# Weight buffers from one tile, handed out by the kernel, and the experts' weights in 2 MB transfers

## The chip, the cores and the metric

The kernel runs on one core of a Trainium2 chip. The metric is the device time of one execution in microseconds (us); the time shown is the median of three runs.

## The reference

The model takes x, one sequence of 256 tokens with 1024 features, in float32, through two blocks of two layers each.

First block, for layer 0 and 1 (ALPHA is the square root of 2):

```
m = conv_mixer(x)  (layer 0)   or   rglru_mixer(x)  (layer 1)
x = layer_norm(ALPHA * x + m, ln1)
f = moe(x)                     # 16 experts, the best 2 of each token, in one of 4 groups
x = layer_norm(ALPHA * x + f, ln2)
```

`conv_mixer` is a product with w_in, two causal depthwise convolutions with gates, and a product with w_out. `rglru_mixer` is u = x w_in, split into a branch y and xr; a causal convolution of 4 taps over xr; two gates, each a block diagonal product of xr; a linear recurrence over the tokens; and (gelu(y) h) w_out. An expert is (silu(x w1) * (x w3)) w2, where w1, w3 and w2 are 1024 x 1024, so an expert has 12 MB of weights, and a layer 192 MB. Every expert's weights are used.

Second block: forgetting attention with 16 heads, a convolutional FFN of width 2816, dilated attention in three groups, the FFN again, and a last rms_norm.

## The kernel before

The 256 tokens stay in SBUF through the whole program, and all the weights, some 547 MB, pass through once. TensorE (PE) works on them in the order of the model: conv mixer, experts of layer 0 (their first product at 117 us), recurrence mixer (from 567), experts of layer 1 (from 678), second block (from about 1135). The order of instructions on each engine is the order in which the kernel's text issues them (a manual schedule): an instruction that waits holds up all that stand behind it on its engine. What a buffer's next writer waits for is the buffer's last reader, by semaphores that the framework places.

Weights. `make_plan` (L352) lists all pieces of 1 MB (128 partitions with a row of 8 KB each) in the order of use. `Ring` (L213) has 19 buffers of one piece each (`SLOTS`), from a tile pool that hands them out in rotation; pieces and larger activations (`take`) share them. `pump` issues the next load on SyncE's queue (SP, L243) as long as a buffer is free in program order; the load itself waits on the chip until the buffer's last reader is done. `reserve` buffers stay free for activations that are yet to come. During the experts, where the parts of `Splitter` aren't needed, their tiles are lent as four pairs of half pieces (`spare`, L236: two loads of 512 KB with rows of 4 KB), and go back and forth until the experts end.

Products outside the experts are split: `Splitter` (L274) makes two parts of each half piece, L293 on ScalarE (ACT) casts the high part and L294 on VectorE (DVE) subtracts for the low part, and PE multiplies three times (L499 to L501). Some pieces are used whole (L495). At most three halves are split ahead.

Experts. `moe` (L1286) sorts tokens by one-hot products. Per expert, stage1 (L1215) reads 8 pieces (w1 and w3, two column halves), stage2 (L1241) the other 4 (w2). Piece n of expert e is key ("moe", l, e, n); `done` frees it after its last reader. Ahead of expert 12 stands a branch for experts with more than 64 tokens (not taken here), which costs PE a jump. The gain and offset of the next norm are spread over the partitions at expert 10 (ln1) and 14 (ln2) into a buffer `gb` (`spread`), which `affine` (L742) later reads on GpSimd (POOL): L745 multiplies by the gain and L746 adds the offset, for each half of the tokens, and then the buffer is dropped.

Between the experts of layer 0 and the recurrence mixer, `go` (L414) takes a buffer for x, three for xT (`split_fm`, L593: the normalized x, feature-major, as two parts and whole) and calls `affine(x, gb, x)`. Then `rglru` begins:

```
            xr, rt, av = view(), view(), view()      # L962: three buffers of the ring
            ...
            conv(products(0))                        # chunks 0 and 1
            conv(products(2))
            pair = products(4)
            conv(pair)
            gates(0)
            gates(1)
```

`products(c)` makes two chunks of 128 columns in PSUM (four tiles `m` in rotation) and L974 on ScalarE writes xr[:, c] from it; `conv` adds three taps to each on VectorE (six L982), then casts (L987, ScalarE) and subtracts (L988, GpSimd); `gates` (L1000 to L1002) needs these and PSUM tiles that the taps have left.

Of the kernel before, what the change touches and what calls it, by code (L numbers as in the profile page):

```python
# [22 lines left out]
SLOTS = 19  # L23
# [32 lines left out]
def wide(w):  # L56
    """[1024, C] -> pieces [2 * C / 512, 128, 4 * 512]: 512 columns, half of the rows."""
# [78 lines left out]
def alibi():  # L136
    """[8, 128, 1152]: per head, the score bias of the three dilated groups."""
# [22 lines left out]
def layout(inp):  # L160
# [52 lines left out]
class Ring:  # L213
    """Slots of 8 KB per partition: weight pieces of 1 MB, loaded in the order in which they are read, and the
    larger activations. `reserve` slots stay free of pieces for activations that are yet to come. `spare`: pairs of
    [128, 1024] tiles that can take the experts' pieces."""

    def __init__(self, nc, pool, plan):
        self.nc, self.pool, self.plan = nc, pool, plan
        self.next, self.used, self.reserve, self.tiles, self.spare = 0, 0, 0, {}, []  # L220

    def slot(self, dtype=F):
        assert self.used < SLOTS
        self.used += 1
        return self.pool.tile([128, 2048], dtype, name="w", tag="w")

    def pump(self):
        while self.next < len(self.plan):
            key, src, n, dst = self.plan[self.next]
            if self.used + self.reserve >= SLOTS:  # L230
                if not self.spare or key is None or key[0] != "moe":
                    break
                self.next += 1
                self.tiles[key] = t = self.spare.pop(0)
                for b in range(2):
                    self.nc.sync.dma_start(t[b], src[:, b * 1024:(b + 1) * 1024])  # L236
# [1716 lines left out]
```

## Time and profile before

| | |
|---|---|
| runs | 1800.62, 1799.11, 1800.96 us; median 1800.62 |
| profiled execution, first to last instruction (its span; no other time of it is given) | 1801.5 us, mean granted TensorE clock 0.986 |
| PE busy | 1739.3 us, 97% of the span, 11892 matmuls |
| VectorE, ScalarE, GpSimd busy | 786.0, 579.5, 210.9 us |
| read from memory | 547.25 MB, 304 GB/s over the span |
| matmuls of the experts, L1215 and L1241 | 366.4 and 181.6 us |
| loads of the experts' pieces | 304 of 1 MB into ring buffers, and the rest in halves of 512 KB |

Busy time is summed over the instructions of an engine; a wait belongs to the engine that stands idle. The share of the DMA is the mean busy share of 16 engines in a stretch. Times within the execution are counted from its first instruction.

### The profile page before, as it was taken

The page shows a single profiled execution, that of the slowest core. Times are in us where ns is not written, and L with a number is a line of the kernel's source. Part 1 is how long each engine was busy: PE and PEld are TensorE (multiplying, and loading weights), DVE is VectorE, ACT ScalarE, POOL GpSimd, SP SyncE. Part 2 cuts the span into 40 slices and gives each one's busy share as a digit, 9 for nine tenths or more (in the row PEclk, how much of TensorE's full clock was granted, in tenths as well). Part 3 has the DMA queues.
Part 4 walks back from the last instruction along what each step waited for, and adds up shares of the span by engine and source line. Part 5 has one row for each costly group of instructions (what it writes and reads, how often), then busy time and mean ns, then how long its engine had stood idle before and what let it go on. Part 6 is the DMA issues. An engine that isn't in the chain of part 4 may idle for free. (4 is left out here: it accounts for less than half of the span.)

```text
span 1801.5 us, 28912 instructions
## 1 busy us (share of the span) xinstructions
PE 1739.3 (97%) x11892; PEld 1252.7 (70%) x11892; DVE 786.0 (44%) x1560; ACT 579.5 (32%) x1065; POOL 210.9 (12%) x211
## 2 busy tenths in 40 slices
PE   9999999998999989999999899899999999999998
PEld 8765555554546975555555454688999989989997
DVE  5841111111115771111111111877877776668776
ACT  5630000010003640000010000555655563456555
POOL 4500000002003300000002000300222200003222
PEclk9999999999999999999999998999999999999999
DMA  9979999999999479999999999626455233665500
GB/s 379 367 296 419 418 421 418 419 418 418 418 419 400 195 302 373 419 419 419 419 418 420 418 416 420 260 85 242 162 190 188 86 121 110 260 259 185 196 1 24
DMA packets 87964, 550.28 MB, mean 305 GB/s; under 512 B 10112, under 2 KB 10112, under 8 KB 31504
## 3 DMA queue, kind: packets, MB, share of 16 engines
q1 hardware_dynamic: 87696, 548.31, 75.6%
q8 instruction: 97, 1.59, 0.3%
q14 instruction: 43, 0.35, 0.1%
q0 software_dynamic: 128, 0.03, 0.0%
HBM read 547.25 MB, written 1.05 MB: 304 GB/s over the span
## 5 line engine op out<-in xcount | busy, mean ns | idle before, releaser
L1215 PE MATMUL m<-w,hi 128*64 128x256 f32 x3264 | 366.4, 381 | 0.0
L294 DVE TENSOR_TENSOR lo<-w,hi 128x1024 fp32r<-128x1024 f32 x238 | 303.5, 1281 | 56.0 <-ACT hi L293 54.8
L1215 PEld LDWEIGHTS m<-w,hi 128*64 128x64 f32 x3264 | 232.3, 137 | 127.8 <-issue 12.3
L499 PE MATMUL m<-w,hi 128*128 128x256 f32 x1104 | 314.4, 285 | 0.0
L500 PE MATMUL m<-w,lo 128*128 128x256 f32 x1104 | 312.7, 283 | 0.5 <-DVE lo L294 0.5
L501 PE MATMUL m<-w,hi 128*128 128x256 f32 x1104 | 312.4, 283 | 0.0
L293 ACT CAST hi<-w 128x1024 fp32r<-128x1024 f32 x232 | 240.0, 1044 | 58.3 <-PE m L501 21.4
L1222 ACT ACTIVATE h<-m 128x256 f32<-128x256 f32 x64 | 24.5, 383 | 680.1 <-PE m L1215 668.9
L1224 DVE TENSOR_TENSOR hs<-h,m 128x256 f32<-128x256 f32 x64 | 26.9, 421 | 435.2 <-ACT h L1222 435.2
L499 PEld LDWEIGHTS m<-w,hi 128*128 128x128 f32 x1104 | 211.8, 192 | 3.8 <-issue 2.1
L500 PEld LDWEIGHTS m<-w,lo 128*128 128x128 f32 x1104 | 211.8, 192 | 2.4 <-DVE lo L294 0.8
L501 PEld LDWEIGHTS m<-w,hi 128*128 128x128 f32 x1104 | 211.8, 192 | 0.0
L1241 PE MATMUL m<-w,ht 128*64 128x512 f32 x800 | 181.6, 604 | 0.2 <-DMA w<-moe 0.2
L1241 PEld LDWEIGHTS m<-w,ht 128*64 128x64 f32 x800 | 55.7, 138 | 109.3 <-issue 104.0
L1403 DVE COPY ys<-m 128x512 f32<-128x512 f32 x30 | 20.7, 692 | 236.1 <-PE m L1241 236.1
L1859 DVE SCALAR_TENSOR_TENSOR t<-u,vecs,t 128x254 f32<-128x254 f32 (+1 forms) x176 | 94.1, 592 | 0.0
L1852 ACT ACTIVATE t<-u,vecs 128x256 f32<-128x256 f32 x88 | 53.0, 602 | 113.4 <-DVE u L1846 110.8
L722 POOL DMA_DIRECT2D w<-rows x4 | 2.4, 598 | 649.5 <-DMA spare<-moe 268.8
L1326 PE MATMUL m<-d,w 128*128 128x128 f32 x512 | 64.6, 288 | 11.5 <-PEq L1348 9.9
L1326 PEld LDWEIGHTS m<-d,w 128*128 128x128 f32 x512 | 62.8, 203 | 13.5 <-issue 11.9
L1846 DVE TENSOR_TENSOR u<-m,w 128x256 f32<-128x256 f32 x84 | 35.4, 422 | 73.1 <-PE m L501 72.8
L1866 POOL TENSOR_TENSOR t<-t,t 128x256 f32<-128x256 f32 x44 | 51.6, 1174 | 123.2 <-ACT t L1865 123.2
(386 smaller groups left out, 2317.1 us busy)
## 6 DMA issues: line engine op xcount, KB each, us to landing
w<-moe SPq DMA_DIRECT2D x304, 1024.0 KB, 16.7
w<-up SPq DMA_DIRECT2D x44, 1024.0 KB, 4.9
lo<-moe SPq DMA_DIRECT2D x72, 512.0 KB, 13.9
hi<-moe SPq DMA_DIRECT2D x54, 512.0 KB, 15.1
w<-down SPq DMA_DIRECT2D x22, 1024.0 KB, 4.8
w<-b_qk SPq DMA_DIRECT2D x12, 1024.0 KB, 4.8
w<-even_in SPq DMA_DIRECT2D x9, 1024.0 KB, 14.0
spare<-moe SPq DMA_DIRECT2D x18, 512.0 KB, 10.1
```

What stands on the lines that cost most here:

```text
L293: (copy or self.nc.scalar.copy)(hi, w)
L294: self.nc.vector.tensor_tensor(lo, w, hi.bitcast(F), op=OP.subtract)
L499: mm(ps, hi[:, k], xT[0][:, k], start=k == 0, stop=False)
L500: mm(ps, lo[:, k], xT[0][:, k], start=False, stop=False)
L501: mm(ps, hi[:, k], xT[1][:, k], start=False, stop=k == 7)
L1215: nc.tensor.matmul(h[f * 64:(f + 1) * 64, j * 256:(j + 1) * 256], xg[:, 4 * i + 2 * b + k], wv[:, k, f], start=i + b + k == 0, stop=i + b ...
L1241: self.nc.tensor.matmul(y[dh * 64:(dh + 1) * 64, :], ht[:, j, f], w[:, dh * 512:(dh + 1) * 512], start=s + j + f == 0, stop=s + j + f == 3)
L1326: nc.tensor.matmul(ps[:, k], x[:, tt, kc], d[:, tt], start=tt == 0, stop=tt == 1)
L1846: nc.vector.tensor_tensor(u, ps, across, op=OP.mult)
L1852: nc.scalar.activation(t, u, AF.Identity, bias=cb[:, ch:ch + 1], scale=cw[:, ch, 2:3])
L1859: nc.vector.scalar_tensor_tensor(t[:, s:], u[:, :256 - s], cw[:, ch, 2 - s:3 - s], t[:, s:], op0=OP.mult, op1=OP.add)
L1866: nc.gpsimd.tensor_tensor(t0, t0, t1, op=OP.mult)
```

## The change

All buffers are now named by the kernel. One tile, the arena, has 15 slots of 8 KB per partition (0 to 14) side by side; slot 15 (`SINGLE`) is a tile of its own; 16 to 19 (`PAIRS`) are two tiles of two slots; 20 to 23 (`SPARE`) stand for the four tiles of `Splitter`, whose two parts now lie in one tile. That is 20 buffers, and four more while they are lent. `take(name)` gives the highest free slot of the arena, or a named slot; xT's two parts go into a pair. Loads go to the first slot in the list of free ones, but `room` holds back the highest `reserve` slots and those in `keep`.

An expert's weights are laid out as 6 blocks of 2 MB with rows of 16 KB instead of 12 of 1 MB. A block goes into two adjacent free slots in one transfer. Where no such pair is free it goes as two halves of 1 MB (`half`), until `settle(True)` at expert 1; after that only into slots that have no partner (`alone`). `settle` also ends the return of lent tiles. The last expert's w2 stays in pieces of 1 MB. Readers see the same 1024 columns at a time as before, through `quarter`, and the order of the matmuls is the same. Comments are removed; the scratch for GpSimd's DMAs has another size.

```diff
-SLOTS = 19
+SLOTS = 15
+SINGLE = 15
+PAIRS = (16, 18)
+SPARE = (20, 21, 22, 23)
...
-    m = np.empty((2, 16, 12, 128, 2048), inp["moe_w1"].dtype)
+    m = np.empty((2, 16, 6, 128, 4096), inp["moe_w1"].dtype)
     for s in range(2):
-        for i in range(2):
-            m[:, :, 4 * s + i] = w1[:, :, s, :, 4 * i:4 * i + 4].reshape(2, 16, 128, 2048)
-            m[:, :, 4 * s + 2 + i] = w3[:, :, s, :, 4 * i:4 * i + 4].reshape(2, 16, 128, 2048)
-            m[:, :, 8 + 2 * s + i] = w2[:, :, s, :, i].reshape(2, 16, 128, 2048)
+        m[:, :, 2 * s] = w1[:, :, s].reshape(2, 16, 128, 4096)
+        m[:, :, 2 * s + 1] = w3[:, :, s].reshape(2, 16, 128, 4096)
+        m[:, :, 4 + s] = w2[:, :, s].reshape(2, 16, 128, 4096)
...
     def __init__(self, nc, pool, plan):
         self.nc, self.pool, self.plan = nc, pool, plan
-        self.next, self.used, self.reserve, self.tiles, self.spare = 0, 0, 0, {}, []
-    def slot(self, dtype=F):
-        assert self.used < SLOTS
-        self.used += 1
-        return self.pool.tile([128, 2048], dtype, name="w", tag="w")
+        self.arena = pool.tile([128, SLOTS * 2048], F, name="w")
+        self.free = list(range(SLOTS + 1)) + [p + i for p in PAIRS for i in range(2)]
+        self.pairs, self.experts, self.lent, self.settled = {}, set(), False, False
+        self.next, self.reserve, self.keep, self.tiles, self.owner = 0, 0, set(), {}, {}
+        self.half = None
+    def lend(self):
+        self.free += SPARE
+        self.lent = True
+        self.pump()
+    def settle(self, on):
+        self.free = [i for i in self.free if i not in SPARE]
+        self.lent, self.settled = False, on
+    def view(self, i, n=1, dtype=F):
+        if i < SLOTS:
+            return self.arena[:, i * 2048:(i + n) * 2048]
+        if i == SINGLE:
+            return self.pool.tile([128, 2048], dtype, name="q", tag="q")
+        if i in SPARE:
+            return self.pool.tile([128, 2048], F, name="s", tag="s", bufs=len(SPARE))
+        p = i - i % 2
+        if p not in self.pairs:
+            self.pairs[p] = self.pool.tile([128, 4096], F, name="r", tag="r", bufs=len(PAIRS))
+        return self.pairs[p][:, i % 2 * 2048:(i % 2 + n) * 2048]
+    def room(self):
+        last = sorted(i for i in self.free if i < SLOTS)
+        last = last[max(0, len(last) - self.reserve):]
+        return [i for i in self.free if i not in last and i not in self.keep]
+    def load(self, key, src, i, n=1):
+        for j in range(i, i + n):
+            self.free.remove(j)
+        t = self.view(i, n)
+        self.nc.sync.dma_start(t[:, :src.shape[-1]], src)
+        self.owner.setdefault(key, []).extend(range(i, i + n))
+        self.tiles.setdefault(key, []).extend(t[:, j * 2048:j * 2048 + 2048] for j in range(n))
+        if key[0] == "moe":
+            self.experts |= set(range(i, i + n))
+    def expert(self, key, src):
+        at = self.room()
+        if self.half is None:
+            for j in at:
+                i = j - j % 2
+                if i in at and i + 1 in at and i != SLOTS - 1 and i not in SPARE:
+                    self.load(key, src, i, 2)
+                    self.next += 1
+                    return True
+        if self.settled:
+            alone = [i for i in at if i in (SLOTS - 1, SINGLE) or i ^ 1 not in self.free and i ^ 1 not in self.experts]
+            at = alone + at if self.half is not None else alone if len(alone) > 1 else []
+        if not at:
+            return False
+        n = 0 if self.half is None else 1
+        self.load(key, src[:, n * 2048:(n + 1) * 2048], at[0])
+        self.half = None if n else key
+        self.next += n
+        return True
     def pump(self):
         while self.next < len(self.plan):
             key, src, n, dst = self.plan[self.next]
-            if self.used + self.reserve >= SLOTS:
-                if not self.spare or key is None or key[0] != "moe":
+            if n == 4096:
+                if not self.expert(key, src):
                     break
-                self.next += 1
-                self.tiles[key] = t = self.spare.pop(0)
-                for b in range(2):
-                    self.nc.sync.dma_start(t[b], src[:, b * 1024:(b + 1) * 1024])
                 continue
-            self.next += 1
             if dst is not None:
                 self.nc.sync.dma_start(dst, src)
-                continue
-            t = self.slot()
-            self.nc.sync.dma_start(t[:, :n], src)
-            self.tiles[key] = t
+            else:
+                at = [i for i in self.room() if i not in SPARE]
+                if not at:
+                    break
+                self.load(key, src[:, :n], at[0])
+            self.next += 1
     def get(self, *key):
         self.pump()
-        return self.tiles[key]
-    def half(self, b, *key):
-        """Half a piece, and what is to be called when its last reader is traced."""
-        t = self.get(*key)
-        return (t[b] if type(t) is tuple else t[:, b * 1024:(b + 1) * 1024],
-                (lambda: self.done(*key)) if b else (lambda: None))
+        return self.tiles[key][0]
+    def half_of(self, b, *key):
+        return self.get(*key)[:, b * 1024:(b + 1) * 1024], (lambda: self.done(*key)) if b else (lambda: None)
+    def quarter(self, b, *key):
+        self.pump()
+        t = self.tiles[key][b // 2]
+        return t[:, b % 2 * 1024:b % 2 * 1024 + 1024], (lambda: self.part(b // 2, key)) if b % 2 else (lambda: None)
+    def part(self, n, key):
+        at = self.owner[key]
+        if n == 0 and (len(at) == 1 or at[0] + 1 != at[1]):
+            self.give(at[0])
+            at[0] = None
+        if n == 1:
+            self.done(*key)
+        self.pump()
+    def give(self, i):
+        self.experts.discard(i)
+        if self.lent or i not in SPARE:
+            self.free.append(i)
     def done(self, *key):
-        t = self.tiles.pop(key)
-        if type(t) is tuple:
-            self.spare.append(t)
-            self.pump()
-        else:
-            self.drop()
-    def take(self, dtype=F):
-        t = self.slot(dtype)
-        self.reserve = max(0, self.reserve - 1)
-        return t
-    def drop(self, n=1):
-        self.used -= n
+        del self.tiles[key]
+        self.drop(key)
+    def take(self, name, slot=None, dtype=F):
+        assert name not in self.owner, name
+        if slot is None:
+            slot = max(i for i in self.free if i < SLOTS)
+            self.reserve = max(0, self.reserve - 1)
+        self.keep.discard(slot)
+        self.free.remove(slot)
+        self.owner[name] = [slot]
+        return self.view(slot, 1, dtype) if slot == SINGLE else self.view(slot)
...
+    def take_pair(self, names, n):
+        p = PAIRS[n]
+        for i, name in enumerate(names):
+            assert name not in self.owner, name
+            self.keep.discard(p + i)
+            self.free.remove(p + i)
+            self.owner[name] = [p + i]
+        self.pairs.pop(p, None)
+        t = self.pool.tile([128, 4096], FR, name="r", tag="r", bufs=len(PAIRS))
+        return t[:, :2048], t[:, 2048:]
+    def drop(self, *names):
+        for name in names:
+            for i in self.owner.pop(name):
+                if i is not None:
+                    self.give(i)
...
-        hi = self.pool.tile([128, 1024], FR, name="hi", tag="hi")
-        lo = self.pool.tile([128, 1024], FR, name="lo", tag="lo")
+        t = self.pool.tile([128, 2048], FR, name="s", tag="s", bufs=len(SPARE))
+        hi, lo = t[:, :1024], t[:, 1024:]
...
-                for i in range(12):
-                    src = a["last"][l, i - 8] if e == 15 and i > 7 else a["moe"][l, e, i]
-                    p.append((("moe", l, e, i), src, 2048, None))
+                for i in range(4 if e == 15 else 6):
+                    p.append((("moe", l, e, i), a["moe"][l, e, i], 4096, None))
+                for i in range(4 if e == 15 else 0):
+                    p.append((("moe", l, e, 8 + i), a["last"][l, i], 2048, None))
...
-        ring.reserve = 5
+            nc.sync.dma_start(ring.tiles[key][0][:, c], src[:, c])
+        ring.reserve, ring.keep = 2, {SINGLE, PAIRS[0], PAIRS[0] + 1}
         ring.pump()
         xf = ring.get("x_fm").rearrange("p (k t) -> p k t", k=8)
-        xT = (ring.take(FR).rearrange("p (k t) -> p k t", k=8), ring.take(FR).rearrange("p (k t) -> p k t", k=8), xf)
+        xT = tuple(t.rearrange("p (k t) -> p k t", k=8) for t in ring.take_pair(("xT0", "xT1"), 0)) + (xf,)
...
+            ring.lend()
             self.resid_ln(acc, x)
-            acc, gb = self.moe(l, x, hi[2], hi[3])
-            x = ring.take().rearrange("p (t d) -> p t d", t=2)
+            acc, gb = self.moe(l, x)
+            self.xname = f"x{l}"
+            x = ring.take(self.xname).rearrange("p (t d) -> p t d", t=2)
...
-        hi, lo = (self.ring.take(FR).rearrange("p (k t) -> p k t", k=8) for _ in range(2))
-        w = self.ring.take().rearrange("p (k t) -> p k t", k=8)
+        hi, lo = (t.rearrange("p (k t) -> p k t", k=8) for t in self.ring.take_pair(("xT0", "xT1"), 0))
+        w = self.ring.take("xT2").rearrange("p (k t) -> p k t", k=8)
...
-        t = self.ring.take().rearrange("p (i d) -> p i d", i=4)
+        t = self.ring.take("gb").rearrange("p (i d) -> p i d", i=4)
...
     def affine(self, x, gb, out):
-        """out = x g + b."""
         for tt in range(2):
             self.nc.gpsimd.tensor_tensor(out[:, tt], x[:, tt], gb[:, 0], op=OP.mult)
             self.nc.gpsimd.tensor_tensor(out[:, tt], out[:, tt], gb[:, 1], op=OP.add)
-        self.ring.drop()
+        self.ring.drop("gb")
...
-                if c == 2:
+                if c == 3:
                     ring.done("x_fm")
...
-            def view():
-                return ring.take().rearrange("p (c t) -> p c t", c=8)
-            xr, rt, av = view(), view(), view()
+            xr, rt, av = (ring.take(n).rearrange("p (c t) -> p c t", c=8) for n in ("xr", "rt", "av"))
...
-            ring.drop(4)
+            ring.drop("xT0", "xT1", "xT2", "xr")
...
+            for b in range(4):
+                w, done = get(b)
+                wv = w.rearrange("p (k f c) -> p k f c", k=2, f=2)
+                for k in range(2):
+                    for f in range(2):
+                        nc.tensor.matmul(h[f * 64:(f + 1) * 64, j * 256:(j + 1) * 256], xg[:, 2 * b + k],
+                                         wv[:, k, f], start=b + k == 0, stop=b + k == 4)
+                done()
...
+                w, done = get(2 * j + f)
...
-            ring.spare.append((spare, rp.tile([128, 1024], F, name="spare")))
-            ring.pump()
-            xT = ring.take().rearrange("p (k t) -> p k t", k=8)
+            xgs = rp.tile([128, 8, 128], F, name="xgs")
+            xT = ring.take("xT").rearrange("p (k t) -> p k t", k=8)
...
-                    return lambda i, b: ring.half(b, "moe", l, e, n + i)
+                    return lambda b: ring.quarter(b, "moe", l, e, n)
...
+                    if e == 1:
+                        ring.settle(True)
+                    if e == 6:
+                        ring.keep = {SINGLE}
                     if e == 8:
-                        ring.reserve = 2
+                        ring.reserve = 1
                     if e == 9:
                         room = self.spread_begin(self.a["rows"][l, :4])
                     if e == 10:
+                        ring.keep = {SINGLE}
                         gb = self.spread(room)
+                    if e == 11:
+                        xa = ring.take("xa", SINGLE).rearrange("p (t d) -> p t d", t=2)
                         ring.reserve = 1
-                    if e == 11:
-                        xa = ring.take().rearrange("p (t d) -> p t d", t=2)
                         self.affine(x, gb, xa)
-                        ring.reserve = 1
                     if e == 13:
-                        ring.reserve = 9 + 2 * l
+                        ring.reserve, ring.keep = 6, {SINGLE, *range(PAIRS[0], PAIRS[l] + 2)}
...
+                        ring.keep.add(SINGLE)
+                        ring.drop("xa")
...
+                        ring.drop(self.xname)
...
-            ring.reserve = 7 + 2 * l
-            ring.spare = []
+            ring.settle(False)
```

## Rows read from the trace of the kernel before

**Rows 1.** Windows: length, busy PE PEld DVE ACT POOL, clock, DMA share, GB/s
```profile
117.00:433.00 316.00, 308.80 (x2254) 170.33 (x2253) 45.83 (x136) 27.48 (x74) 10.06 (x5) 1.00 1.00 414
678.00:995.00 317.00, 310.02 (x2254) 170.81 (x2251) 42.64 (x112) 27.46 (x74) 9.94 (x5) 0.99 1.00 414
1135.00:1801.00 666.00, 654.63 (x4537) 591.02 (x4535) 490.35 (x872) 360.42 (x592) 104.84 (x101) 1.00 0.42 154
```

**Rows 2.** Waits of PE: line waited for, total us, times, longest us
```profile
PE m L1326 <- PEq L1348: 9.9, 2, 5.1
PE m L1000 <- DVE w L982: 3.1, 1, 3.1
PE m L1241 <- DMA w<-moe: 0.2, 1, 0.2
```

**Rows 3.** Timeline (start, us): PE, last weights of expert 11, layer 0
```profile
429.98 1.51 PE L1241 MATMUL m<-w,ht 128*64 128x512 f32 x6 [0.22 <-DMA w<-moe]
```

**Rows 4.** Timeline of POOL: the affine ahead of the recurrence mixer
```profile
571.60 2.36 POOL L745 TENSOR_TENSOR w<-w 128x1024 f32<-128x1024 f32 x1
574.03 3.22 POOL L746 TENSOR_TENSOR w<-w 128x1024 f32<-128x1024 f32 x1
577.22 2.36 POOL L745 TENSOR_TENSOR w<-w 128x1024 f32<-128x1024 f32 x1
579.66 3.27 POOL L746 TENSOR_TENSOR w<-w 128x1024 f32<-128x1024 f32 x1
```

**Rows 5.** Timeline of ACT at the beginning of the recurrence mixer
```profile
571.37 0.56 ACT L974 ACTIVATE w<-m,vecs 128x256 f32<-128x256 f32 x1
571.83 1.04 ACT L293 CAST hi<-w 128x1024 fp32r<-128x1024 f32 x1
```

**Rows 6.** Timeline of DVE in the recurrence mixer
```profile
572.90 2.14 DVE L294 TENSOR_TENSOR lo<-w,hi 128x1024 fp32r<-128x1024 f32 x1 [1.85 <-ACT hi L293]
583.94 2.42 DVE L982 SCALAR_TENSOR_TENSOR w<-m,vecs,w 128x255 f32<-128x255 f32 x6
590.38 2.42 DVE L982 SCALAR_TENSOR_TENSOR w<-m,vecs,w 128x255 f32<-128x255 f32 x6
```

**Rows 7.** Timeline of PE in the recurrence mixer
```profile
566.77 14.08 PE L495 MATMUL m<-w 128*128 128x256 f32 x64 [0.26 <-ACT w L600]
580.50 0.47 PE L499 MATMUL m<-w,hi 128*128 128x256 f32 x1
592.56 0.36 PE L1000 MATMUL m<-xh,hi 128*128 128x256 f32 x1 [3.11 <-DVE w L982]
```

**Rows 8.** Windows: 8 KB rows, 4 KB rows; part 6: a lone load
```profile
231.00:271.00 40.00, 39.43 (x292) 22.28 (x290) 4.66 (x13) 3.98 (x11) 0.00 (x0) 1.00 1.01 421
164.00:172.00 8.00, 8.00 (x56) 3.76 (x54) 0.69 (x1) 0.00 (x0) 0.00 (x0) 1.00 1.03 408
w<-b_qk SPq DMA_DIRECT2D x12, 1024.0 KB, 4.8
```

**Rows 9.** Timeline of PE, experts 1, 3 and 11 of layer 0
```profile
163.59 5.32 PE L1241 MATMUL m<-w,ht 128*64 128x512 f32 x24
202.68 1.51 PE L1215 MATMUL m<-lo,hi 128*64 128x256 f32 x12
424.38 5.37 PE L1241 MATMUL m<-w,ht 128*64 128x512 f32 x24
```

**Rows 10.** Timeline of SP and PE, layer 1: experts 1, 3, 9, 11
```profile
672.73 37.02 SPq L243 DMA_DIRECT2D w<-moe  x17
724.59 5.32 PE L1241 MATMUL m<-w,ht 128*64 128x512 f32 x24
754.38 1.90 PE L1215 MATMUL m<-w,hi 128*64 128x256 f32 x16
910.60 1.03 PE L1215 MATMUL m<-hi 128*64 128x256 f32 x8
987.07 7.09 PE L1241 MATMUL m<-w,ht 128*64 128x512 f32 x32
```

More of the change, by code (lines that the diff above doesn't have):

```diff
@@ L434, in go @@
         self.ring = ring = Ring(nc, wp, plan)
-        self.sw = sw
-        self.split = Splitter(nc, ring, sw, keys, whole)
+        self.split = Splitter(nc, ring, wp, keys, whole)
         nc.scalar.preload_act_table(AF.Sigmoid)
         for key in (("x_fm",), ("even_in", 0)):
-            ring.tiles[key] = ring.slot()
+            ring.tiles[key] = [ring.take(key)]
         for key, src, h in ((("even_in", 0), self.a["even_in"][0], 0), (("x_fm",), self.a["x_fm"], 0),
@@ L607, in split_fm, with split_raw @@
         return hi, lo, w
-    def split_raw(self, chunks, g):
+    def split_raw(self, chunks, g, n=0):
         nc = self.nc
         gv = self.vec(g)
-        hi, lo = (self.ring.take(FR).rearrange("p (k t) -> p k t", k=8) for _ in range(2))
+        hi, lo = (t.rearrange("p (k t) -> p k t", k=8)
+                  for t in self.ring.take_pair((("xT0", "xT1"), ("yT0", "yT1"))[n], n))
         def step(k, ps):
@@ L718, in spread_begin @@
     def spread_begin(self, src):
-        room = self.ring.take()[:4].rearrange("p (i d) -> p i d", i=4)
+        room = self.ring.take("room", SINGLE)[:4].rearrange("p (i d) -> p i d", i=4)
         rows, sels = room[:, 0], room[:, 1].rearrange("p (i c) -> p i c", i=4)
@@ L738, in spread @@
                 nc.scalar.copy(t[:, j], ps)
-        self.ring.drop()
+        self.ring.drop("room")
         return t.rearrange("p (i h) d -> p i (h d)", i=2)
@@ L788, in conv_mixer @@
         with self.pool("cw", bufs=3) as wk:
-            ca = view(ring.take())
+            ca = view(ring.take("ca"))
             sq, cv = ca[:, :4], ca[:, 4:]
@@ L1346, in moe @@
                         nmax = nc.values_load(ci, min_val=0, max_val=T)
-                        stage = ring.take()
+                        stage = ring.take("stage")
                         with tc.If(nmax > CAP):
@@ L1472, in attn_a @@
         with self.pool("aw", bufs=2) as wk:
-            both = ring.take().bitcast(BF)
+            both = ring.take("both").bitcast(BF)
             cq, ck, part = (both[:, i * 1024:(i + 1) * 1024].rearrange("p (c t) -> p c t", c=4) for i in range(3))
-            v = ring.take().rearrange("p (t d) -> p t d", t=2)
+            v = ring.take("v0").rearrange("p (t d) -> p t d", t=2)
             room = [v[:, i, 512:].rearrange("p (c t) -> p c t", c=2) for i in range(2)], part
-            ot = tuple(ring.take(FR).rearrange("p (c t) -> p c t", c=8) for _ in range(2))
+            ot = tuple(t.rearrange("p (c t) -> p c t", c=8) for t in ring.take_pair(("ot0", "ot1"), 1))
             acc = self.accs()
@@ L1555, in attn_a @@
             self.v_proj(acc, "a_v", xT, 0)
-            ring.drop()
+            ring.drop("xT2")
             r = self.inv_rms(x, fp)
@@ L1586, in attn_a @@
                 if i == 6:
-                    ring.reserve = 3
-                    ring.drop(2)
+                    ring.reserve, ring.keep = 1, set(range(PAIRS[0], PAIRS[0] + 2))
+                    ring.drop("xT0", "xT1")
                     acc = self.accs()
@@ L1609, in attn_a @@
                 pass
-            ring.drop(5)
+            ring.drop("both", "v0", "ot0", "ot1", "carve")
         return acc
@@ L1702, in attn_b @@
         split.hold = False
-        xT, steps = self.split_raw(chunks, "mix1")
+        xT, steps = self.split_raw(chunks, "mix1", 1)
         with self.pool("bw", bufs=2) as wk:
-            v = [ring.take()[:, :1536] for _ in range(2)]
-            ot = ring.take(FR).rearrange("p (s c t) -> p s c t", s=2, c=4)
-            qks = [ring.take()[:, :1536].rearrange("p (c t) -> p c t", c=6) for _ in range(2)]
+            v = [ring.take(n)[:, :1536] for n in ("v0", "v1")]
+            ot = ring.take("ot0", SINGLE, FR).rearrange("p (s c t) -> p s c t", s=2, c=4)
+            qks = [ring.take(n)[:, :1536].rearrange("p (c t) -> p c t", c=6) for n in ("qk0", "qk1")]
             acc = self.accs()
@@ L1791, in attn_b @@
                 else:
-                    ring.reserve = 3
-                    ring.drop(4)
+                    ring.reserve, ring.keep = 1, set(range(PAIRS[0], PAIRS[0] + 2))
+                    ring.drop("xT0", "xT1", "yT0", "yT1")
                     acc = self.accs()
@@ L1826, in ffn @@
         with self.pool("ff", bufs=2) as wk:
+            self.ring.keep = set() if l else {SINGLE, PAIRS[1], PAIRS[1] + 1}
             acc = self.accs()
@@ L1895, in ffn @@
                 if j == 12:
[L1896 removed]
+                    self.ring.reserve = 0 if l else 4
             split.advance()
@@ L1905, in ffn @@
             self.out_last(acc, [gs[NJ - 2], gs[NJ - 1]], w)
-            self.ring.reserve += 3
-            self.ring.drop(3)
+            self.ring.reserve += 1
+            if not l:
+                self.ring.keep |= {PAIRS[0], PAIRS[0] + 1}
+            self.ring.drop("xT0", "xT1", "carve")
         return acc
@@ L1914, in __init__ @@
     def __init__(self, ring):
-        self.slot, self.at = ring.take(), 0
+        self.slot, self.at = ring.take("carve"), 0
     def tile(self, shape, dtype, name=None, tag=None, bufs=1):
```

67 lines of the change are left out of this document (24 added, 43 removed).

## The prediction

> **What bounds the kernel now.** I read the table of windows first, then the waits of PE, then the timelines of the two places where the change reorders work. The windows [rows 1] show both mixtures of experts with PE busy 98% of the time at the full granted clock while the DMA share is 1.00; in the second transformer (1135 to 1801) PE is as busy and the DMA share is 0.42, so the loads there have room. The waits [rows 2] say that in both mixtures together PE lost 0.2 us to a load, and 9.9 us to the two jumps over the untaken branch ahead of expert 12. So PE sets the end, and the experts' weights come just in time: the one wait is at 429.98, for the last piece of expert 11 [rows 3]. The lead that the buffers hold when the experts begin is eaten during eleven experts and is zero at their end; what the jump takes gives it back. Two questions follow: does any PE input come later after the change, and is the lead eaten faster?
>
> **Part 1: who gets which slot.** Before, the pool hands out buffers in rotation; now `take` gives the highest free slot of the arena. At expert 14 of layer 0 every slot from 8 to 14 is free (`reserve` is 6), so `gb` gets 14. Then x0 gets 13 and xT2 12. `affine(x, gb, x)` drops `gb` in program order, at once, while GpSimd still has to read it; `reserve` is 3, so nothing is loaded into 14, and the next `take`, the recurrence mixer's `xr`, gets 14. ScalarE's first L974 writes xr's chunk 0, 256 columns inside gb's gain half (the first 1024), which is read by the two multiplications L745. That write must now wait for the second of them, which ran from 577.22 to 579.58 [rows 4]; before, the L974 ran at 571.37 [rows 5].
>
> Behind it in ScalarE's queue stand L293 (the cast for odd_in 2) and the next L974; VectorE's queue waits for that cast with L294, and behind that stand the six conv taps L982; PE's fifth chunk (L499) needs the parts of odd_in 2 and a PSUM tile that the taps free. Step by step: GpSimd's addition took 3.22 us and its multiplication, of the same shape, 2.36, while VectorE worked beside them; VectorE will now be idle there, so I take 2.4 for each, and the second L745 ends at 571.60 + 3 x 2.4 = 578.8. L974 then runs at 578.9, the cast (0.5 after it, 1.04 long) ends at 580.4, L294 beside the last addition takes the 2.14 of [rows 6] and ends at 582.5, six taps in 2.42 end at 584.9. PE's own products end at 566.77 + 14.08 = 580.85 [rows 7], its fifth chunk started at 580.50 in the overlap, and now starts at 584.9: a gap of 4 us. The rest goes by rounds: from the end of one set of taps (583.94 + 2.42 = 586.36) to the end of the next (592.80) is 6.44 us, in which PE waits for VectorE as it does now. Two rounds behind 584.9 end at 597.8, against 592.80, and gates(1) starts some 0.2 us ahead of that. Loose work in the first round (casts that could run ahead before and can't now) adds about 0.2. Sum: 5.2 us. Bounds: 0 if the write doesn't wait; 9.3 if it waited for the whole affine (579.66 + 3.27 = 582.93, that is 4.1 later than 578.8). The late mixer end moves everything behind it; no slack lies there, because PE is at 98% in the next stage too.
>
> With GpSimd no faster than it was (579.58) the sum would be 6.0. The Trainium skill (SBUF — State Buffer, Who interferes with whom) says that a VectorE instruction with two inputs in SBUF contends with a GpSimd instruction that reads SBUF. By it the same shape taking 2.36 and 3.22 us in [rows 4] is the doing of VectorE's work beside it, and the sum is 5.2; by the rows as they stand it is 6.0.
>
> The same pattern in layer 1 costs nothing: attention takes its slots before `affine` drops gb.
>
> **Part 2: the experts' weights in 2 MB.** Rates: 8 KB rows ran at 421 GB/s, 4 KB rows at 408 [rows 8]: 2.49 and 2.57 us per MB (1.0486e6 bytes). Halving the number of rows once gained 0.08 us; if the cost is by row, halving again gains 0.04, so 2 MB take 4.90 us. Bounds: 4.98 (no gain) and 4.82 (the whole 0.08 again). I take 4.90. The bytes are the same, PE's instructions are the same: per expert PE needs (910.60 - 754.38)/6 = 26.0 us [rows 10] and the DMA 29.4 (29.9 before), so the lead is still eaten by 3.4 us per expert.
>
> The Trainium skill (DMA: Bandwidth & Descriptors, Specifications) gives 435 GB/s as the fabric's ceiling. 2 MB would then take 4.82 us, the lower bound that the rows give anyway; its memory limit of 358 GB/s is not what this trace shows.
>
> What the lead is worth depends on the slots. I walked the new allocator by hand with the release times of this trace. Until expert 1 is traced pieces go as 1 MB halves into any free slot, the four lent buffers too. Then `settle` ends the lending, and a transfer wants two adjacent free slots. In layer 0 the pieces of expert 1's fourth and fifth transfer sit in the lent buffers, which don't come back; the stream is unbroken until 163.3, and the next adjacent pair (12 and 13) comes free with expert 1's last weights, read until 168.9 [rows 9]. First byte to landing adds 2.3 us (a lone 1 MB load lands after 4.8 us [rows 8], of which 2.5 are transfer), and a transfer counts only when all its 2 MB have landed: the DMA idles about 7.8 us. That pair lands at 176.0 and is used at 202.68, 26.7 early. From there to the last transfer of expert 11 are 51 transfers, 51 x 4.90 = 249.9, landing at 425.9; it is first read 16 matmuls into the 24 that start at 424.38 [rows 9], at 427.9. So 2 us of lead are left: no stall. At 4.98 it is 2.1 late.
>
> In layer 1 the issue starts after xT is free, at 672.73 [rows 10], and 13 MB follow at 2.49 from 682 to 714.5. Then x0 in slot 13 spoils the pair 12, 13; the first adjacent pair (10 and 11) comes free near 728.0, within the last weights of expert 1 (724.59 + 5.32). The DMA idles 15.8 us. This pair lands at 735.2 and is used at 754.38: 19.2 early, 7.5 less than in layer 0. 36 transfers on, 176.4 us, expert 9's first lands at 911.6, 1.0 after its use at 910.60. 17 more transfers take 83.3 us while PE needs 987.07 + 3.55 - 910.60 = 80.0: 3.3 more. Stall 4.4 us in experts 9 to 11. At 4.98 it is 3.9 + 4.7 = 8.6, with layer 0 10.7 in all; at 4.82 it is 0. Below zero there is nothing to gain, since PE waited 0.2 us. After the jump the lead is back, as now.
>
> **Part 3: the rest, at nothing.** The extra buffer replaces 4 MB of lent pairs that came back before and don't now; its worth is inside the walk. The view of a quarter and the loop over four change no instruction on PE. `xgs` in its own tile and `xa` in its own buffer are taken at the same points, and their writers (GpSimd, off the path) have tens of us. x_fm is freed one chunk later; what that holds back is a load of the experts' weights, first read at 117 [rows 1]. If that cover is gone it costs one load, 2.5 us.
>
> **Sum.** Against the profiled execution's span of 1801.5: 5.2 + 0 + 4.4 = 9.6, 1811.1. The median of the runs is 1800.6, 0.9 below this execution, so 1810.2. I predict 1810.
>
> **Rivals.**
> A. The mixer's wait as above, but the stream keeps up: 2 MB in 4.82 us, or a pair free a few us earlier. For it: 4.90 is half way between bounds, and 0.04 per MB already halves the stall. Against: it needs the full second gain. Time: 1800.6 + 5.2 = 1805.8. It is also what the page's ceiling would give.
> B. The rows gain nothing, 4.98: 10.7 in the mixtures. For it: a queue that is full at 1.01 share may be limited elsewhere than in rows. 1800.6 + 5.2 + 10.7 = 1816.5.
> C. The other side: the slot order isn't as I walked it. Both losses come from that one walk: `xr` in another slot than gb, and a pair free when the stream needs it. It decides at one slot: if gb, x0 or one expert's piece stands one place off, 14 is not xr's and the pairs don't break. Then the 2% better rate keeps the lead, and nothing is lost: 1800.6, within 1 us. Against: 14 is the highest slot and free at both takes.
> D. The change doesn't do what it says: few pairs form, halves of 1 MB remain, or 16 KB rows are slower than 8 KB ones. At the 4 KB rate, 5.14 per transfer, the stall passes 20 us: above 1820.
>
> **Chances.** Forecast (1806 to 1815) 0.39, A 0.18, B 0.15, C 0.21, D 0.07. 0.2% is 3.6 us, about what a measurement can tell from no change here. The forecast, B and D lie above 1804.2 (0.61), and A but for a sixth of it, where the mixer loses less (0.15). C is centred on no change and a little under a third of it, where something in its favour went unseen, is below 1797. Faster 0.06, same 0.15 + 0.03 = 0.18, slower 0.76. The range 1799 to 1818 holds the forecast, A, B and most of C; out are D and C's lower part, 0.13. The forecast's own range is 1806 to 1815.
>
> **What would show it.** Right: ScalarE's first L974 starts near 579 with a wait for GpSimd's L745; PE has a gap of about 4 us near 581 to 585; gates(1) is 5 us late; the DMA moves about 428 GB/s inside the mixtures, with an idle stretch of 8 us at 163 to 171 and of 16 us at 714 to 730 (720 to 735 after the mixer's loss); PE waits for loads of the experts 9 to 11 of layer 1, some 4 us. Wrong: L974 at 571; no idle DMA behind expert 0; PE waiting for loads in layer 0, which would mean B or D; or a new wait in the second transformer, where I expect none.

## The result, and the profile after

The changed kernel takes 1815.62 us (median of five runs, 1814.57 to 1817.27), against 1800.96 for the kernel before in the same session; ratio 1.0069, 95% interval 1.0051 to 1.0087. A second round gave 1.0061 (1.0036 to 1.0086). By the ratios it is slower by 11 to 12 us, while the medians lie 14.7 us apart: runs of the kernel before alone spread from 1797 to 1808 us, so a single pair of medians, or of spans (1801.5 and 1812.9), can be off by several us, and the text below goes by the ratios. 1810 was forecast, range 1799 to 1818; 1815.62 lies in that range, 0.6 us above the 1806 to 1815 that the forecast proper allowed, and next to rival B's 1816.5.

Lines have other numbers in the changed kernel: stage1 and stage2 of the experts (L1215, L1241) are L1304 and L1330, the jump's L1326 and L1348 are L1413 and L1435, the mixer's L499, L974, L982 and L1000 are L591, L1064, L1072 and L1090, the affine's L745 and L746 are L838 and L839, and the splitter's L293 and L294 are L387 and L388.

First the waits of PE after the change (line waited for, us in total, times, longest):

```profile
PE m L1413 <- PEq L1435: 10.0, 2, 5.1
PE m L1364 <- DVE g L1363: 4.9, 4, 1.2
PE m L1304 <- DMA w<-moe: 4.1, 5, 1.2
PE m L591 <- DVE w L1072: 3.4, 1, 3.4
PE m L1330 <- DMA w<-moe: 2.5, 3, 1.2
PE m L1330 <- DMA r<-moe: 1.7, 1, 1.7
PE m L1090 <- DVE w L1072: 1.5, 1, 1.5
```

Against [rows 2]: the 0.2 us for loads have become 8.3, and ahead of L591 (the former L499, the mixer's fifth chunk) stands a new wait of 3.4. The jump costs the same.

The mixer, ScalarE first, then GpSimd, VectorE and PE (timelines: start, length):

```profile
573.79 1.28 ACT L1053 ACT_TABLE_LOAD   x1
582.42 0.56 ACT L1064 ACTIVATE w<-m,vecs 128x256 f32<-128x256 f32 x1 [7.34 <-POOL w L838]
582.89 1.03 ACT L387 CAST s<-r 128x1024 fp32r<-128x1024 f32 x1
```

```profile
575.32 2.34 POOL L838 TENSOR_TENSOR w<-w 128x1024 f32<-128x1024 f32 x1
577.74 2.35 POOL L839 TENSOR_TENSOR w<-w 128x1024 f32<-128x1024 f32 x1
580.04 2.35 POOL L838 TENSOR_TENSOR w<-w 128x1024 f32<-128x1024 f32 x1
582.47 2.36 POOL L839 TENSOR_TENSOR w<-w 128x1024 f32<-128x1024 f32 x1
```

```profile
583.95 1.96 DVE L388 TENSOR_TENSOR s<-r,s 128x1024 fp32r<-128x1024 f32 x1 [9.19 <-ACT s L387]
591.12 1.22 DVE L388 TENSOR_TENSOR s<-r,s 128x1024 fp32r<-128x1024 f32 x1 [0.18 <-ACT s L387]
```

```profile
570.49 14.08 PE L587 MATMUL m<-w 128*128 128x256 f32 x64 [0.32 <-ACT w L692]
588.01 0.55 PE L591 MATMUL m<-r,s 128*128 128x256 f32 x1 [3.44 <-DVE w L1072]
600.88 0.36 PE L1090 MATMUL m<-xh,s 128*128 128x256 f32 x1 [1.46 <-DVE w L1072]
```

ScalarE sits 7.34 us behind its table load until the second multiplication of the affine ends at 582.38, and writes 0.04 us later. The additions take 2.35 us, not the 3.22 of [rows 4]. VectorE is idle beside the first; beside the second, which had begun, it is VectorE's L388 that is held up (1.96 us, against 1.22 where GpSimd is idle). Counted from the start of the affine, which lies 3.7 us later here, the first write moved from -0.2 (571.37) to 7.1 us, PE's fifth chunk from 8.9 to 12.7, gates(1) (L1090 at 600.88) from 21.0 to 25.6.

The stream of weights, in windows (columns as in [rows 1]):

```profile
160.00:175.00 15.00, 15.00 (x109) 8.32 (x109) 2.06 (x5) 1.77 (x5) 0.00 (x0) 1.00 0.59 225
720.00:745.00 25.00, 25.00 (x192) 14.82 (x188) 3.42 (x9) 2.88 (x8) 0.00 (x0) 1.00 0.44 173
200.00:428.00 228.00, 225.14 (x1628) 124.57 (x1626) 30.15 (x81) 20.15 (x54) 10.07 (x5) 0.99 1.01 426
765.00:985.00 220.00, 212.11 (x1526) 117.29 (x1522) 28.38 (x76) 18.66 (x50) 9.94 (x5) 0.99 1.01 426
```

The DMA share falls to 0.59 and 0.44 in the two stretches behind expert 0: 6 and 14 us idle, where PE is still fully busy. Afterwards it runs without a gap, and PE pays later, in layer 0 some 260 us behind the idle stretch, in layer 1 from some 170 us on (timeline of PE, waits in brackets; layer 0, then layer 1):

```profile
429.85 3.65 PE L1330 MATMUL m<-w,ht 128*64 128x512 f32 x16 [0.95 <-DMA w<-moe]
...
897.32 3.67 PE L1304 MATMUL m<-w,xgs 128*64 128x256 f32 x32 [1.00 <-DMA w<-moe]
917.37 3.65 PE L1330 MATMUL m<-r,ht 128*64 128x512 f32 x16 [1.68 <-DMA r<-moe]
922.25 3.67 PE L1304 MATMUL m<-w,xgs 128*64 128x256 f32 x32 [1.24 <-DMA w<-moe]
927.07 3.67 PE L1304 MATMUL m<-w,xgs 128*64 128x256 f32 x32 [1.14 <-DMA w<-moe]
1005.47 3.65 PE L1330 MATMUL m<-w,ht 128*64 128x512 f32 x16 [1.24 <-DMA w<-moe]
```

With four shorter ones they sum to 7.6 us in experts 8 to 11 of layer 1, and 0.95 in layer 0 (8.6 in all; the list above has 8.3, as one of 0.2 stands in a line of its own that is not shown).

### The profile page after: what moved, and what is told of

It reads as the page before. It is cut to its first block, busy times and chain, and to the rows that moved or that the text cites. A ratio compares the mean times of both kernels' runs of the same rounds, so it can differ in the third digit from the quotient of the medians.

```text
span 1812.9 us, 28454 instructions
## 1 busy us (share of the span) xinstructions
PE 1742.8 (96%) x11892; PEld 1256.9 (69%) x11892; DVE 781.0 (43%) x1560; ACT 579.1 (32%) x1065; POOL 209.5 (12%) x211
## 5 line engine op out<-in xcount | busy, mean ns | idle before, releaser
L1304 PE MATMUL m<-w,xgs 128*64 128x256 f32 x3088 | 349.0, 381 | 4.1 <-DMA w<-moe 4.1
L591 PE MATMUL m<-r,s 128*128 128x256 f32 x1104 | 315.4, 286 | 3.4 <-DVE w L1072 3.4
L592 PE MATMUL m<-r,s 128*128 128x256 f32 x1104 | 313.7, 284 | 0.0
L593 PE MATMUL m<-r,s 128*128 128x256 f32 x1104 | 313.5, 284 | 0.0
L1304 PEld LDWEIGHTS m<-w,xgs 128*64 128x64 f32 x3088 | 220.3, 137 | 127.3 <-issue 15.3
L388 DVE TENSOR_TENSOR s<-w,s 128x1024 fp32r<-128x1024 f32 x208 | 263.8, 1273 | 48.9 <-ACT s L387 47.7
L387 ACT CAST s<-w 128x1024 fp32r<-128x1024 f32 x204 | 211.2, 1044 | 54.6 <-PE m L593 21.3
L591 PEld LDWEIGHTS m<-r,s 128*128 128x128 f32 x1104 | 212.9, 193 | 7.6 <-issue 5.9
L592 PEld LDWEIGHTS m<-r,s 128*128 128x128 f32 x1104 | 212.9, 193 | 1.6
L593 PEld LDWEIGHTS m<-r,s 128*128 128x128 f32 x1104 | 212.9, 193 | 0.0
L1330 PE MATMUL m<-w,ht 128*64 128x512 f32 x688 | 157.6, 605 | 2.5 <-DMA w<-moe 2.5
L1330 PEld LDWEIGHTS m<-w,ht 128*64 128x64 f32 x688 | 48.6, 139 | 97.4 <-issue 95.2
L1304 PE MATMUL m<-r,xgs 128*64 128x256 f32 x848 | 98.7, 385 | 0.2 <-DMA r<-moe 0.2
L1304 PEld LDWEIGHTS m<-r,xgs 128*64 128x64 f32 x848 | 60.6, 139 | 34.4 <-issue 3.9
L1413 PE MATMUL m<-d,w 128*128 128x128 f32 x512 | 64.5, 288 | 11.7 <-PEq L1435 10.0
```

What stands on the lines that cost most here:

```text
L387: (copy or self.nc.scalar.copy)(hi, w)
L388: self.nc.vector.tensor_tensor(lo, w, hi.bitcast(F), op=OP.subtract)
L591: mm(ps, hi[:, k], xT[0][:, k], start=k == 0, stop=False)
L592: mm(ps, lo[:, k], xT[0][:, k], start=False, stop=False)
L593: mm(ps, hi[:, k], xT[1][:, k], start=False, stop=k == 7)
L1304: nc.tensor.matmul(h[f * 64:(f + 1) * 64, j * 256:(j + 1) * 256], xg[:, 2 * b + k], wv[:, k, f], start=b + k == 0, stop=b + k == 4)
```

## The experiments

Ratios are to the kernel before, with 95% intervals; 0.1% is 1.8 us.

**rt ahead of xr.**

```diff
-            xr, rt, av = (ring.take(n).rearrange("p (c t) -> p c t", c=8) for n in ("xr", "rt", "av"))
+            rt, xr, av = (ring.take(n).rearrange("p (c t) -> p c t", c=8) for n in ("rt", "xr", "av"))
```

> The changed kernel, but the recurrence mixer takes rt ahead of xr, so rt gets slot 14 (gb's) and xr gets slot 11. Theory: xr's first write waits for GpSimd's second multiplication by gb; rt is first written some 30 us later, so the wait goes. ScalarE's first L1064 starts about 1 us behind the table load instead of 7.3 us, PE's fifth chunk starts at the end of the first four, and the execution is 3 to 5 us shorter than the changed kernel, near 1812; the waits for loads in the experts stay (about 8 us in layer 1). Rival: the mixer is late for what GpSimd and VectorE do anyway (the affine was in the way before, too), and the time stays at 1815.

Measured: 1810.13 us, 1.0038 (1.002 to 1.0055): 5.6 us less than the changed kernel. ScalarE's timeline:

```profile
572.41 1.28 ACT L1053 ACT_TABLE_LOAD   x1
573.70 0.56 ACT L1064 ACTIVATE w<-m,vecs 128x256 f32<-128x256 f32 x1
```

No wait is left, and none on PE ahead of the fifth chunk; the waits for loads stay (7.9 us). Which of three buffers gets gb's slot decides the mixer's loss.

**The lent buffers kept.**

```diff
-                    if e == 1:
-                        ring.settle(True)
```

> The changed kernel without settle at expert 1: the lent buffers keep coming back, and pieces may go on as 1 MB halves into any free slot. Theory: the loss in the experts is the stretch in which the DMA idles after expert 0 (4 buffers gone, and a pair to wait for); without it some 370 of the experts' loads are 1 MB loads at about 2.48 us, so a slower stream than 4.90 us for 2 MB, yet PE waits for no load, margins of 8 to 10 us are left at expert 11, and the time falls by 8 to 10 us to about 1806. Rival: the loss is the rate of the stream (hiccups in it, rows); then this kernel, with the smaller rows, loses as much or more: 1815 or above.

Measured: 1803.66 us, 1.0004 (0.9987 to 1.0021): 12 us less. PE waits for no weights of stage1 or stage2. The windows show the DMA without a hole, and 8 KB rows at 421 GB/s where the changed kernel had 426:

```profile
720.00:745.00 25.00, 25.00 (x186) 14.61 (x184) 3.84 (x10) 2.88 (x8) 0.00 (x0) 1.00 1.01 419
765.00:985.00 220.00, 217.72 (x1577) 120.63 (x1575) 29.73 (x80) 19.01 (x51) 9.92 (x5) 0.99 1.01 421
```

So a slower stream without the hole loses nothing; the rival falls.

**Halves, without the lent buffers.**

```diff
-                        ring.settle(True)
+                        ring.settle(False)
```

> The changed kernel with the lending ended at expert 1 as there, but with halves of 1 MB allowed on. It parts the idle stretch in two: the four buffers that don't come back, and the wait for two adjacent slots. Theory: by the walk the DMA idles 5 us in layer 0 and less than 10 in layer 1, margins at expert 11 are 3.5 and 7 us, PE waits for no load: about 1806 as with the lent buffers kept. If the missing buffers are the cause, PE still waits several us and the time is 1810 or more.

Measured: 1804.67 us, 1.0000 (0.9983 to 1.0017); no wait for weights. The window:

```profile
720.00:745.00 25.00, 25.00 (x190) 14.74 (x186) 3.42 (x9) 2.88 (x8) 0.00 (x0) 1.00 0.92 365
```

A share of 0.92 is a hole (an idle stretch of the DMA) of 2 us instead of 14. Most of the hole was the wait for two adjacent slots, not the four missing buffers.

**Each 2 MB as two loads.**

```diff
-        self.nc.sync.dma_start(t[:, :src.shape[-1]], src)
+        for c in range(0, src.shape[-1], 2048):
+            w = min(2048, src.shape[-1] - c)
+            self.nc.sync.dma_start(t[:, c:c + w], src[:, c:c + w])
```

> The changed kernel, same slots and same order, but each 2 MB transfer issued as two of 1 MB with 8 KB rows. It shows what the 16 KB rows are worth by themselves. Theory: 2 MB take 4.97 instead of 4.90 us, 53 of them in a row in each layer lose 3.7 us more, less up to 1.7 us because the first half can be used when it has landed: PE's waits for loads grow from 10 to about 13 to 15 us in both layers, time about 1818 to 1820. Rival: bigger transfers have no rate of their own, or the later landing of whole 2 MB is what costs; then the time is the same or 2 us shorter than the changed kernel.

Measured: 1815.26 us, 1.0074 (1.0051 to 1.0096), the same as the changed kernel. The rate is that of 8 KB rows, and the hole is shorter (windows):

```profile
720.00:745.00 25.00, 25.00 (x194) 15.06 (x192) 3.07 (x8) 2.88 (x8) 0.00 (x0) 1.00 0.55 207
765.00:985.00 220.00, 214.41 (x1528) 117.12 (x1526) 28.39 (x76) 18.66 (x50) 9.93 (x5) 0.98 1.01 421
```

PE's waits for loads are 6.3 us, not 13 to 15. A miss: 421 against 426 GB/s costs 0.06 us per 2 MB, 3 us in a layer, and it is made up elsewhere. One part the windows show: the DMA share in 720 to 745 is 0.55 instead of 0.44, so the hole is 2.8 us shorter: a first half lands at 727.43, well ahead of its second half at 740.48. The other, which no run separates, is that the first half is usable half a transfer earlier at each wait; I had credited this 1.7 us at most, and the shorter hole nothing.

**Both edits (rt first, lent buffers kept).**

> The changed kernel with both edits that each gave time back: rt taken ahead of xr, and no settle at expert 1 (lent buffers come back, halves of 1 MB go on). Theory: the two losses are independent, one in the recurrence mixer and one in the loads of the experts, so the gains add: no wait of ScalarE on GpSimd, no wait of PE for the experts' weights, and a time some 5 us below that of the kernel with only the lent buffers kept, at or a little under the kernel before (ratio 0.996 to 1.000). Rival: they overlap (a later mixer start gives the loads time and hides part of the other), and the ratio stays at 1.000 or above.

Measured: 1798.87 us, 0.997 (0.9957 to 0.9983): 6 us below the lent buffers alone. The gains add.

**The mixer's wait put into the kernel before.**

```diff
-                acc = self.rglru(xT)
+                acc = self.rglru(xT, gb)
...
-    def rglru(self, xT):
+    def rglru(self, xT, gb):
...
             xr, rt, av = view(), view(), view()
+            xr = gb.rearrange("p i d -> p (i d)").rearrange("p (c t) -> p c t", c=8)
```

> The kernel before with one thing of the change alone: the recurrence mixer's xr is put into gb's buffer (the buffer that it would have had stays unused for that time). Theory: the same wait as in the changed kernel: ScalarE's first L974 starts near 579, after GpSimd's second multiplication; PE's fifth chunk is 4 us late; the execution is 4 to 6 us longer than before, ratio 1.002 to 1.0035. Rival: the mixer's lateness in the changed kernel comes from something else in it (the pair tile of xT, the split parts in one tile); then no difference here.

Measured: 1806.08 us, 1.0014 (0.9999 to 1.003): 2.5 us more, below what was expected; the interval reaches from no difference into the range expected (1.002 to 1.0035), so the time alone doesn't decide. Its trace has the mechanism (ScalarE's timeline):

```profile
578.86 0.56 ACT L975 ACTIVATE w<-m,vecs 128x256 f32<-128x256 f32 x1 [7.35 <-POOL w L745]
```

PE waited 2.6 us ahead of the fifth chunk, and 2.6 ahead of gates(1), where before it was 3.1 alone [rows 2]. Gates(1) starts 30.4 us behind the mixer's first product here, as in the changed kernel, and 25.8 in the kernel before.

**settle at expert 4, with rt first; and settle at expert 4 alone.**

```diff
-                    if e == 1:
+                    if e == 4:
                         ring.settle(True)
```

> The changed kernel with rt ahead of xr, and settle(True) at expert 4 instead of 1: halves until then, afterwards 2 MB transfers with 16 KB rows as in the change. Theory: what cost time in the experts was not the 2 MB transfers but that the search for pairs began while the slots were still scattered and the DMA idled; by the walk begun at expert 4 it leaves no idle stretch, the last weights of expert 11 land 8 us early in layer 0 and 10 in layer 1, PE waits for no load, and the time is that of the kernel with halves throughout: 0.996 to 1.000 of before. Rival: the larger transfers themselves cost (whole 2 MB must land); then waits of some us stay in experts 9 to 11 and the ratio is about 1.003, as with rt first alone.

> The changed kernel with one number changed, settle at expert 4 instead of 1; xr still waits for gb. Theory: PE waits for no load of the experts, the mixer's loss stays: 4 to 5 us above the version with rt first as well, ratio 0.998 to 1.001 and some 12 us below the changed kernel. Rival: the two losses overlap, and this alone gives all of it back (0.996).

Measured: with rt first 1797.07 us, 0.9959 (0.9944 to 0.9974); alone 1802.96, 1.0005 (0.9991 to 1.002). The windows of the first:

```profile
720.00:745.00 25.00, 24.43 (x179) 12.67 (x177) 2.47 (x6) 2.15 (x7) 0.00 (x0) 1.00 1.01 419
765.00:985.00 220.00, 217.15 (x1566) 119.68 (x1564) 28.78 (x77) 19.73 (x53) 9.93 (x5) 0.99 1.01 426
```

No hole, 426 GB/s in 2 MB transfers, and no wait for weights. The 2 MB transfers by themselves cost nothing here; beginning the search for pairs at expert 1 did. (Settling at expert 4 also keeps the lent buffers until then, but the halves above show that their lack alone costs no wait.) The two differ by 0.46% (8 us), more than the mixer's loss elsewhere, within the intervals. The version with both beats the kernel before by 0.4%.

**The kernel before and the changed one again.**

> The kernel before against itself: what a ratio of 1 looks like here, and a second trace, to see which of the stretches in which TensorE runs at half its clock recur. Theory: the execution times of one kernel spread over some 10 us because these stretches come and go, so the ratio is within 0.2% of 1, while the trace has some of them elsewhere than the first one (1082 to 1086, 594 to 597). Rival: they are tied to the code and stand in the same places.

> The changed kernel once more, with a second trace. Theory: the wait of ScalarE on GpSimd (7.3 us, PE 3.8 us late), the idle DMA behind expert 0 of both layers and PE's 8 us of waits for loads recur to within 1 us, ratio 1.006 to 1.008; the half-clock stretches differ. Rival: part of the 8 us (4 were forecast) was this one trace's bad luck in the stream; then the waits are nearer to 4 to 5 us here.

Measured: before against itself 0.9994 (0.9977 to 1.001), span 1805.4; the changed kernel 1.0061, span 1811.4, with 8.3 us of waits for loads and a wait of 7.33 us of ScalarE on L838. Both recur to 0.1 us. What moves is TensorE's granted clock, between its two levels of 2.4 and 1.2 GHz. Examples are the four-row products of the spread (8 matmuls each) in both traces of the kernel before, at expert 14 of layer 0 (first trace, then second) and of layer 1 (first trace):

```profile
518.68 3.77 PE L734 MATMUL m<-w 4*128 4x512 f32 x8
```

```profile
521.42 5.99 PE L734 MATMUL m<-w 4*128 4x512 f32 x8
```

```profile
1080.77 6.04 PE L734 MATMUL m<-w 4*128 4x512 f32 x8
```

Their mean granted clocks are 0.96, 0.60 and 0.60 of the full one. So the first place ran mostly at the upper level once and mostly at the lower once; the other was slow in both traces (6.02 us, 0.60 in the second), and took 3.71 us at 0.98 in the second trace of the changed kernel. Neither "tied to the code" nor "random" holds for all of them; why remains open.

## Why the prediction was right, and where it was off

Direction, range and both mechanisms were right; the loss was 10 us forecast and 11 to 12 measured. Two of the prediction's own marks went the other way. The measured 1815.6 is nearer to rival B's number than to the forecast's, though B's reason (rows that gain nothing) is not what the traces show. And PE did wait for a load in layer 0 (0.95 us), which was named as a sign of B or D; what made it is the term of the experts below.

**The mixer, 5.2 us.** gb and xr shared slot 14. The write came 7.1 us behind the affine's start (forecast 7.3), the fifth chunk 12.7 (13.3), gates(1) 4.6 us late (5.2). The traces agree on this better than the times do: from the mixer's first product to gates(1) it is 30.39 to 30.43 us in all seven traces in which xr has gb's buffer (the changed kernel twice, lent buffers kept, halves, two loads, settle at 4 alone, and the kernel before with that one edit), and 25.73 to 25.79 in the five in which it hasn't. By times: 5.6 us (rt first against the changed kernel), 6.1 (both edits against lent buffers), 8.3 (settle at 4, with and without) and 2.5 (in the kernel before); their mean is 5.6, each with some 4 us of uncertainty. The term stands, 0.6 us too large. A step not foreseen is on the clock: within the 3.4 us in which PE had no work its granted clock fell, to 0.50 from 587.0 to 593.8, so the fifth chunk and the beginning of the sixth ran at the lower level (0.41 us a matmul in the timeline, against 0.28 afterwards). That is paid out of PE's wait at gates(1) (1.5 us in this trace, 2.6 in the second), because VectorE's taps set when gates(1) starts. The slow stretch that the kernel before had behind gates(1) was absent in this trace.

On the additions I weighed the rows as they stood (6.0) against the rule of the Trainium skill (SBUF — State Buffer, Who interferes with whom) that GpSimd reads contend with VectorE's second input: the trace sides with the rule, 2.35 us for each of four, and 3.22 and 3.26 again for the additions where VectorE is busy beside them, in the version with rt first and settle at 4.

**The experts, 0 + 4.4 us.** The walk gave the slots, the pairs and both holes (7.8 and 15.8 us; 6 and 14 by the windows). The term that was mis-sized is the rate of the whole stream: I took 4.90 us for each 2 MB, from the best 40 us of the kernel before. A single transfer takes that (most landings in the trace of the changed kernel are 4.89 or 4.90 us apart), but the 53 transfers' worth from the first pair of layer 1 (landed at 742.64) to the last of expert 11 (1005.33) took 4.956 each. In every trace some landings, one to six in a layer, are late by 0.3 to 1.7 us; why is open. The windows of [rows 1] (414 GB/s, against 421 in [rows 8]) held them, together with the slower 4 KB rows, and I made nothing of the difference. 51 to 53 times 0.056 is 3.0 us a layer: the lead of 2 in layer 0 became a wait of 0.95, the stall of 4.4 in layer 1 became 7.6. The sum of 8.6 is nearer to rival B's 10.7 than to 4.4, but by late landings and not for B's reason: 16 KB rows do gain, 426 against 421. By times the experts' loss is 11 to 12 us (three kernels without it: 1.0004, 1.0000 and 1.0005, against 1.0069), with some 4 us of uncertainty, so the 8.6 of the trace lie within it.

**The rest, nothing.** One thing was missed. xa, the normalized x that the experts' sum takes in at expert 13, now has its own buffer, free at once, and the affine that writes it starts 24 us earlier in layer 0 (381.36 instead of 405.78) and 13 in layer 1. Before, it ran beside VectorE's L1274 at expert 11 (timeline of VectorE, two operations in a row, first the kernel before, then the changed one, both in layer 1):

```profile
976.01 2.31 DVE L1274 TENSOR_SCALAR g<-csts,pos,gate 128x128 f32<-128x128 f32 x2
```

```profile
990.28 0.60 DVE L1363 TENSOR_SCALAR g<-csts,pos,gate 128x128 f32<-128x128 f32 x2
```

PE waited for this operation 6.9 us in the kernel before, 4.9 now (5.7 in the second trace). The 1.2 to 2.0 us are a gain that the forecast lacked. Why the two mended versions with rt first pass the kernel before by 5 to 7 us isn't shown. It is hardly the waits: PE is idle 60.8 and 61.2 us of their spans, against 62.2 and 60.5 in the two traces of the kernel before. What differs is the time in which it is busy, 1736.4 and 1735.0 us against 1739.3 and 1744.9 for the same 11892 matmuls, and so the clock; whether the change has a part in that is open.

By the trace, then: 4.6 + 8.6 - 2.0 = 11.2, against 11.4 between the spans. The agreement is partly luck, since the clock's slow stretches, which differ by several us between two traces of one kernel, are not in it. Stage by stage it doesn't hold: from the first product of layer 0's experts to the mixer the changed kernel's trace is 3.3 us longer, where the waits give about nothing; from there to layer 1's experts 3.0 (4.6 by the waits), and from there to the second block 4.7 (6.6).

## What to carry to other kernels

When buffers get fixed addresses, ask of each "highest free" or "first free" choice whose last reader it inherits, and on which engine's queue that wait will stand; a buffer written late is the one to give the slot still being read. A policy that waits for a better-shaped slot pays when the transfer queue runs dry, and the bill may come 170 or 260 us later, where the lead runs out. Rate a long stream by its mean over the whole stretch, not by its best window. And where times of one kernel spread by more than the effect, measure between two fixed instructions of the traces: the mixer's 4.6 us, lost in 4 us of uncertainty by the times, recurs there within 0.1 us.

## What the runs showed of the hardware that was not expected

Rows of 16 KB moved 426 GB/s over 220 us (the changed kernel), rows of 8 KB 421 (two loads), a mix of 8 and 4 KB 419 (window 200 to 428 of the kernel before). Two VectorE operations with one tensor input each (L1274) took 2.31 instead of 0.60 us beside GpSimd; the Trainium skill (SBUF — State Buffer, Who interferes with whom) puts `tensor_scalar` among those that can block so, and this trace agrees.
